# Short convolution's sum and normalised rows kept in PSUM banks, and the low weight parts of one stage fixed on GpSimd

## The chip, the cores and the metric

The kernel runs on one core of a Trainium2 chip. The metric is the device time of one execution in microseconds; the median of several runs is compared. The engines are TensorE (PE), VectorE (DVE), ScalarE (ACT), GpSimd (POOL) and SyncE (SP), which issues most loads. SBUF is the working memory; PSUM has eight banks, each of 128 partitions x 512 float32, into which TensorE writes.

## What is computed

The reference is a block of two layers on 256 tokens with 1024 features, in float32. Only its first stage matters here. Cut to that:

```python
h = rms_norm(x, norm_mix_g)                        # 256 x 1024
proj = h @ w_in                                    # 1024 -> 7168
sc_b, sc_c, sc_x, cf_a, cf_g, gate_sc, gate_cf = split(proj)
y_sc = (sc_b * causal_depthwise_conv(sc_c * sc_x, sc_conv_w)) @ sc_w_out     # short: 3 taps
cf = (cf_a + b1) * sigmoid(cf_g + b2)
cf = silu(layer_norm(causal_depthwise_conv(cf, cf_conv_w) + cf_conv_b))      # long: 31 taps
y_cf = cf @ cf_w_pw2 + cf_b_pw2
x = x + (sigmoid(gate_sc) * y_sc + sigmoid(gate_cf) * y_cf) @ w_mix_out
mem_n = rms_norm(mem, norm_mem_g)                  # keys and values of a cross attention
```

Cross attention, a feed-forward part over 16384 experts and a second block with two attentions follow. All of this is unchanged in the code.

## The kernel before

**Units.** Features lie on the 128 partitions and the 256 tokens along the row. A weight matrix is cut into units of 128 x 1024 float32 (512 KB). A unit is loaded by SP into `w` (three buffers, L322), rounded by ScalarE to a high part `wh` (L288), and the rest, `wl` = `w` - `wh`, is made by GpSimd or VectorE (L292, in `split_gen`). The moving rows are split in the same way into a high and a low part. A product takes 24 matmuls of 128 columns by 256 tokens (`go`, L370 in `blk`): 16 with `wh` and 8 with `wl`. `wh` and `wl` have three buffers each, so the split of a unit waits for the end of the unit three before it.

**Order of the work.** TensorE's order is the order in which the program calls `go`. Everything else is a generator that yields operations, each with an engine, a planned cost and what it depends on. A planner (`Sched`) keeps a planned time for every engine and writes the instructions out one after another; where an operation names two engines (`either`: VectorE or GpSimd) it takes the one that is planned to end first, with a bias added. For `wl` the bias is -2000 ns for GpSimd unless the unit names another. The order is fixed when the program is built, and each engine then runs its own instructions in that order.

**The first stage.** The 56 units of `w_in` come in this order: a and g of the long convolution in turn for j = 0 to 7; then triples c, x, b of the short convolution for j = 0 to 7, with six units of `w_v` (`go_v`, L800 to L804) after the third triple; then the gates gs and gc, 16 units. The first units (j < 4) take `x` times its gain, and their result is multiplied by the row factor `R0` afterwards; from j = 4 on they take the normalised row `hN`. Eight units of `sc_w_out`, eight of `w_k` and eight of `cf_w_pw2` follow.

**The short convolution.** `post_c` copies the c unit's result to `scc` on ScalarE. `post_x` multiplies the x unit's bank by it into `scx` (SBUF, L238), then makes the sum over three taps in `scy` (SBUF): a tensor_scalar (L659) and two products-and-sums (scalar_tensor_tensor, L662), all on VectorE. `post_b` multiplies the b unit's bank by `scy`; ScalarE takes the high part `eA` of it and VectorE the low part `eB`.

**Normalised rows.** `prep_n` and `prep_mem` multiply one of eight tiles of the input or of the memory by its row factor into `mt` (SBUF, two buffers; `either`), and `hl_gain` makes from it the high part on ScalarE and the low part on VectorE (L479): `hN` and `memHL`. They run in two lanes of four tiles.

**Beside it.** The long convolution (`conv_gen`) is 31 steps for each of eight tiles on VectorE, L603 for the first and L607 for the others, with the running sum in a bank; it has a low priority and fills VectorE's planned free time. `layer_norm` adds its tiles up (L717, L739) and needs matmuls with ones (L460 has the same for the row factors `R0` and `Rm`, from square sums `sqT`).

**Banks.** Two pools of four banks each: `mmb` for the results of units, `msb` for the rest. Before the change the first stage uses `msb` for the long convolution (`conv_bank`), for the layer norm's sums (`ln_bank`) and for three later results of the layer norm.

The planned costs that the change exchanges are these, in ns:

```python
def c_dve(n, ap=0, fast=False):
    return 66 + n / (1.92 if fast else 0.96) + 60 * ap
def c_psum(n, ap=0):
    return 130 + n / 0.96 + 40 * ap
```

Of the kernel before, what the change touches and what calls it, by code (L numbers as in the profile page):

```python
# [19 lines left out]
F32 = mybir.dt.float32  # L20
# [5 lines left out]
OP = mybir.AluOpType  # L26
# [4 lines left out]
S = 256  # L31
# [147 lines left out]
# [6 lines that stand above are left out]
# [16 lines left out]
def tile_kernel(ctx, tc, A, out):  # L201
# [24 lines left out]
    def once(pool):  # L226
        b = []

        def f():
            if not b:  # L230
                b.append(pool())
            return b[0]

        return f


    def tt(o, a, b, op):
        return lambda e="dve": ENG[e].tensor_tensor(o, a, b, op=op)  # L238
# [14 lines left out]
    def vcol(name, j=0, w=1):  # L253
        return vec[:, VC[name] + j:VC[name] + j + w]
# [81 lines left out]
    def add(src, **kw):  # L336
        u = dict(src=src, i=len(units), **kw)
        units.append(u)
        return u
# [136 lines left out]
    def hl_gain(H, L, src, g, n, hev, lev, deps=()):  # L476
        yield Op("act", c_act(n, 1), act(H, src, AF.Copy, scale=g), deps=deps, ev=hev)
        yield Op("dve", c_dve(n, 1),
                 lambda: V.scalar_tensor_tensor(L, src, g, H.bitcast(F32), op0=OP.mult, op1=OP.subtract), ev=lev)  # L479
# [77 lines left out]
        yield from rstd(sqT[:, 0], Rm, (), "Rm", bank=mmb)  # L557

    def prep_mem(k):
        t = T1.tile([128, S], F32, tag="mt", bufs=2, name="mt")  # L560
        yield Op(either(S), tt(t, mem[:, k], Rm, OP.mult), deps=["Rm"])
        yield from hl_gain(memHL[:, 0, k], memHL[:, 1, k], t, vcol("norm_mem_g", k), S, None, ("mem", k))

    def mem_part(c):

# [76 lines left out]
    scx, scc = {}, {}  # L642
# [8 lines left out]
    def post_x(j):  # L651
        def g(p):
            b = T1.tile([128, 2 + S], F32, tag="scx", bufs=2, name="scx")
            y = T1.tile([128, S], F32, tag="scy", bufs=3, name="scy")
            scx[j] = y
            yield Op("pool", 40.0, lambda: POOL.memset(b[:, 0:2], 0.0))
            yield Op("dve", c_dve(S), tt(b[:, 2:2 + S], p[:, :S], scc[j], OP.mult), deps=[("scc", j)])
            yield Op("dve", c_dve(S, 1, True),
                     lambda: V.tensor_scalar(y, b[:, 0:S], vcol("sc_w", j * 3), None, op0=OP.mult))  # L659
            for k in (1, 2):  # L660
                yield Op("dve", c_dve(S, 1),
                         lambda k=k: V.scalar_tensor_tensor(y, b[:, k:k + S], vcol("sc_w", j * 3 + k), y,  # L662
                                                            op0=OP.mult, op1=OP.add),
                         ev=("scy", j) if k == 2 else None)
        return g

# [16 lines left out]
    cfHL = P1.tile([128, 2, 8, S], FR, tag="cfHL", name="hN")  # L683

    def prep_n(k):
        t = T1.tile([128, S], F32, tag="mt", bufs=2, name="mt")
        yield Op(either(S), tt(t, x[:, k], R0, OP.mult), deps=["R0"])
        yield from hl_gain(cfHL[:, 0, k], cfHL[:, 1, k], t, vcol("norm_mix_g", k), S, None, ("hn", k))

# [15 lines left out]
    def layer_norm():  # L705
        M0 = T1.tile([128, S], F32, tag="R", bufs=3, name="M0")
        Rl = T1.tile([128, S], F32, tag="R", bufs=3, name="Rl")
        acc = T1.tile([128, S], F32, tag="acc", name="accl")

        def sum1():  # L710
            return ln_bank()[:, 0:S]

        def sum2():
            return ln_bank()[:, S:2 * S]

        for j in range(1, 7):
            yield Op("dve", c_psum(S), lambda j=j: V.tensor_tensor(  # L717
                acc if j == 6 else sum1(), cc[:, j], cc[:, 0] if j == 1 else sum1(), op=OP.add),
                deps=[("cc", 0), ("cc", j)])
        b, c = [None], [None, None]  # L720

        def f():
            b[0] = msb()
            PE.matmul(b[0][:, :S], onesD, acc, start=True, stop=True)

        yield Op("pe", 430.0, f)
        yield Op("act", c_act(S), lambda: ACT.activation(M0, b[0][:, :S], AF.Copy, scale=8.0 / 7.0), ev="M0")
        yield Op("act", c_act(S), lambda: ACT.activation(b[0][:, :S], b[0][:, :S], AF.Copy, scale=8.0 / 7.0))
        acc2 = T1.tile([128, S], F32, tag="acc", name="acc2")
        t7 = T1.tile([128, S], F32, tag="mt", bufs=2, name="t7")  # L730
        sq0 = T1.tile([128, S], F32, tag="t", bufs=4, name="sq0")
        for j in range(8):
            t = t7 if j == 7 else T1.tile([128, S], F32, tag="cfa", bufs=3, name="cm")
            yield Op("dve", c_psum(S), lambda t=t, j=j: V.tensor_tensor(t, cc[:, j], b[0][:, :S], op=OP.subtract),
                     deps=[("cc", j)], chain=False, ev="t7" if j == 7 else None)
            sq = sq0 if j == 0 else T1.tile([128, S], F32, tag="sq", bufs=2, name="sq")
            yield Op("act", c_act(S), act(sq, t, AF.Square), ev="sq0" if j == 0 else None)
            if j:
                yield Op("dve", c_psum(S), lambda j=j, sq=sq: V.tensor_tensor(  # L739
                    acc2 if j == 7 else sum2(), sq, sq0 if j == 1 else sum2(), op=OP.add))  # L740

        def f1():
            c[0], c[1] = msb(), msb()
            ln["mu"], ln["R"] = c[0][:, :S], c[1][:, :S]
            PE.matmul(c[0][:, :S], onesD, t7, start=True, stop=True)
            PE.matmul(c[1][:, :S], onesD, acc2, start=True, stop=True)

        yield Op("pe", 860.0, f1)
        d2 = T1.tile([128, S], F32, tag="cfa", bufs=3, name="d2")
        yield Op("act", c_act(S), lambda: ACT.activation(d2, c[0][:, :S], AF.Square), chain=False)  # L750
        yield Op("dve", c_psum(S), lambda: V.tensor_tensor(d2, c[1][:, :S], d2, op=OP.subtract))
        yield Op("dve", c_psum(S), lambda: V.tensor_tensor(c[0][:, :S], M0, c[0][:, :S], op=OP.add), chain=False,
                 ev="mu")
        yield Op("act", 310.0, lambda: ACT.activation(Rl, d2, AF.Sqrt, bias=epsc[:, 0:1]))
        yield Op("dve", 1670.0, lambda: V.reciprocal(c[1][:, :S], Rl), ev="Rl")
        yield Op("act", 1400.0, lambda: ACT.activation(junk, epsc[:, 0:1], AF.Silu), chain=False)
# [69 lines left out]
        order += [("a", j), ("g", j)]  # L826
    tiles0 = {"b": 0, "c": 8, "x": 16, "a": 24, "g": 32, "gs": 40, "gc": 48}
    for key, j in order:
        u_in[key, j] = add(W["w_in"][tiles0[key] + j])
    VAT, NV1 = 9, 3  # L830
    u_v = []
    order2 = []
# [3 lines left out]
    for i, (key, j) in enumerate(order2):  # L836
        if i == VAT:
            u_v += [add(W["w_v"][n]) for n in range(2 * NV1)]
        u_in[key, j] = add(W["w_in"][tiles0[key] + j])
    u_sc = [add(W["sc_w_out"][n]) for n in range(8)]  # L840
    u_k = [add(W["w_k"][n]) for n in range(8)]
    u_cf = [add(W["cf_w_pw2"][n]) for n in range(8)]
# [1268 lines left out]
```

## Time and profile before

| | us |
|---|---|
| median of 3 runs (lowest, highest) | 1807.87 (1806.69, 1808.79) |
| the profiled execution, its own time | 1811.32 |
| its span, first to last instruction | 1809.5 |
| TensorE busy, matmuls | 1688.5 (93%) |
| VectorE busy | 1222.8 (68%) |
| ScalarE busy | 803.3 (44%) |
| GpSimd busy | 1185.9 (66%) |

All times in the rows are microseconds from the span's start unless they are marked ns; "x8" is a count. An arrow in a tile's name reads "output <- inputs", and "<-ACT wh L288" behind idle time names what ended it. The mean granted TensorE clock of the whole execution is 0.954 of full speed.

### The profile page before, as it was taken

The page shows a single profiled execution, that of the slowest core. Times are in us where ns is not written, and L with a number is a line of the kernel's source. Part 1 is how long each engine was busy: PE and PEld are TensorE (multiplying, and loading weights), DVE is VectorE, ACT ScalarE, POOL GpSimd, SP SyncE. Part 2 cuts the span into 40 slices and gives each one's busy share as a digit, 9 for nine tenths or more (in the row PEclk, how much of TensorE's full clock was granted, in tenths as well). Part 3 has the DMA queues.
Part 4 walks back from the last instruction along what each step waited for, and adds up shares of the span by engine and source line. Part 5 has one row for each costly group of instructions (what it writes and reads, how often), then busy time and mean ns, then how long its engine had stood idle before and what let it go on. Part 6 is the DMA issues. An engine that isn't in the chain of part 4 may idle for free.

```text
span 1809.5 us, 33154 instructions
## 1 busy us (share of the span) xinstructions
PE 1688.5 (93%) x13460; PEld 1666.1 (92%) x13460; DVE 1222.8 (68%) x1994; ACT 803.3 (44%) x1302; POOL 1185.9 (66%) x509
## 2 busy tenths in 40 slices
PE   8898989898996999999999999999999889979997
PEld 7898989898996999999999999999999878979997
DVE  7999966658998706776006777889787897474302
ACT  5533445555443442222443223444444545656533
POOL 5677865456685884444884556887688633768885
PEclk8999999999998998888999999999999999999999
DMA  6454644445453453222553334555455331545553
GB/s 200 151 175 146 192 163 141 129 129 165 148 182 115 150 179 115 94 94 94 171 180 117 115 117 129 186 180 161 152 186 181 120 102 65 165 139 176 185 187 117
DMA packets 75305, 266.73 MB, mean 147 GB/s; under 512 B 8720, under 2 KB 9232, under 8 KB 75152
## 3 DMA queue, kind: packets, MB, share of 16 engines
q1 hardware_dynamic: 73856, 262.77, 44.8%
q8 instruction: 105, 1.72, 0.4%
q10 hardware_dynamic: 1296, 1.85, 0.3%
q14 instruction: 48, 0.39, 0.1%
HBM read 262.48 MB, written 2.10 MB: 146 GB/s over the span
## 4 chain that ended last, share of the span: by engine, by line
PE 61%; DVE 33%; ACT 3%; issue 2%; DMA 1%; POOL 0%; SPq 0%; DVEq 0%; ACTq 0%; POOLq 0%
PE mmb L370 29%; PE msb L1343 7%; PE msb L1341 7%; PE msb L1345 7%; DVE msb L607 5%; PE msb L1264 4%; PE mmb L1264 4%; DVE zz L238 3%; DVE scr L1182 1%; DVE scy L662 1%; DVE scr L1143 1%; DVE scr L1140 1%; ACT wh L288 1%; DVE scr L1179 1%; DVE scr L1142 1%
## 5 line engine op out<-in xcount | busy, mean ns | idle before, releaser
L292 POOL TENSOR_TENSOR wl<-w,wh 128x1024 fp32r<-128x1024 f32 x473 | 1162.2, 2461 | 591.4 <-ACT wh L288 413.3
L288 ACT ACTIVATE wh<-w 128x1024 fp32r<-128x1024 f32 x491 | 518.4, 1059 | 587.9 <-PE msb L1343 260.1
L238 DVE TENSOR_TENSOR zz<-Ah,zz 128x256 fp32r<-128x256 f32 x128 | 216.4, 1693 | 140.0 <-ACT zz L241 140.0
L370 PE MATMUL mmb<-hA,wh 128*128 128x256 f32 x1024 | 263.8, 293 | 1.2 <-ACT wh L288 1.2
L370 PE MATMUL mmb<-hB,wh 128*128 128x256 f32 x1024 | 262.1, 291 | 0.0
L1343 PE MATMUL msb<-zz,wh 128*128 128x256 f32 x1008 | 252.1, 287 | 7.8 <-DVE zz L238 7.7
L1341 PE MATMUL msb<-zz,wh 128*128 128x256 f32 x1008 | 253.2, 288 | 0.8 <-ACT zz L241 0.8
L370 PEld LDWEIGHTS mmb<-hA,wh 128*128 128x128 f32 x1024 | 206.6, 202 | 1.4 <-ACT wh L288 1.4
L370 PEld LDWEIGHTS mmb<-hB,wh 128*128 128x128 f32 x1024 | 205.6, 201 | 0.0
L1343 PEld LDWEIGHTS msb<-zz,wh 128*128 128x128 f32 x1008 | 197.1, 196 | 8.8 <-DVE zz L238 8.8
L1341 PEld LDWEIGHTS msb<-zz,wh 128*128 128x128 f32 x1008 | 197.2, 196 | 1.0 <-ACT zz L241 1.0
L370 PE MATMUL mmb<-hA,wl 128*128 128x256 f32 x1024 | 156.3, 299 | 0.4 <-POOL wl L292 0.4
L1345 PE MATMUL msb<-zz,wl 128*128 128x256 f32 x1008 | 145.0, 287 | 0.0
L370 PEld LDWEIGHTS mmb<-hA,wl 128*128 128x128 f32 x1024 | 142.1, 205 | 0.6 <-POOL wl L292 0.6
L370 PE MATMUL mmb<-hN,wh 128*128 128x256 f32 x896 | 120.4, 286 | 13.3 <-ACT hN L241 5.5
L1345 PEld LDWEIGHTS msb<-zz,wl 128*128 128x128 f32 x1008 | 132.3, 195 | 0.0
L1264 PEld LDWEIGHTS <-ohF 128*128 128x128 f16 x1024 | 121.5, 146 | 11.2 <-DVE ohF L1256 6.0
L370 PEld LDWEIGHTS mmb<-hN,wh 128*128 128x128 f32 x896 | 113.2, 195 | 15.3 <-ACT wh L288 6.7
L607 DVE SCALAR_TENSOR_TENSOR msb<-glu,vec,msb 128x256 f32<-128x256 f32 x232 | 113.1, 487 | 6.2
L1268 DVE SCALAR_TENSOR_TENSOR Ah<-msb,Ah 128x512 f32<-128x512 f32 x32 | 22.1, 692 | 101.3 <-PE msb L1264 101.3
L1234 ACT ACTIVATE Ah<-mmb 128x256 f32<-128x256 f32 x128 | 47.1, 368 | 84.0 <-PE mmb L370 84.0
L370 PE MATMUL mmb<-eu,wh 128*128 128x256 f32 x512 | 70.7, 287 | 6.4 <-DVE uHL L474 2.7
(465 smaller groups left out, 3268.1 us busy)
## 6 DMA issues: line engine op xcount, KB each, us to landing
w<-in_peer_u_dram SPq DMA_DIRECT2D x128, 512.0 KB, 3.5
w<-in_peer_v_dram SPq DMA_DIRECT2D x128, 512.0 KB, 3.5
w<-in_w_in_dram SPq DMA_DIRECT2D x81, 512.0 KB, 3.5
w<-in_w_up_dram SPq DMA_DIRECT2D x32, 512.0 KB, 3.5
w<-in_w_down_dram SPq DMA_DIRECT2D x32, 512.0 KB, 3.5
w<-in_w_peer_q_dram SPq DMA_DIRECT2D x16, 512.0 KB, 3.7
w<-in_w_v_dram SPq DMA_DIRECT2D x8, 512.0 KB, 3.5
w<-in_sc_w_out_dram SPq DMA_DIRECT2D x8, 512.0 KB, 3.6
```

Source lines behind the costliest of these rows:

```text
L238: return lambda e="dve": ENG[e].tensor_tensor(o, a, b, op=op)
L288: yield Op("act", c_act(1024), lambda: ACT.activation(h, w, AF.Copy), deps=u["wdep"], ev=("H", u["i"]))
L292: lambda e: ENG[e].tensor_tensor(l, w, h.bitcast(F32), op=OP.subtract), ev=("L", u["i"]))
L370: PE.matmul(p[:, :S], a, b, start=first and n == 0, stop=last and n == len(todo) - 1)
L607: lambda k=k: V.scalar_tensor_tensor(cc[:, j] if k == 30 else o(), glu[:, j, k:k + S], vcol("cf_w", j * 31 + k), o(), op0=OP.mult, op1=OP. ...
L662: lambda k=k: V.scalar_tensor_tensor(y, b[:, k:k + S], vcol("sc_w", j * 3 + k), y, op0=OP.mult, op1=OP.add),
L1234: yield Op("act", c_act(S), lambda: ACT.activation(Ah[n // 64][:, n % 64], p[:, :S], AF.Gelu), ev=("U", n))
L1264: PE.matmul(b[0][:, t * 64:(t + 1) * 64], ohJ[:, :, t], gI[i][:, :, t], start=i == 0, stop=i == 1)
L1268: yield Op("dve", c_dve(512), lambda: V.scalar_tensor_tensor(z, b[0].rearrange("p (t i) -> p i t", t=8), 1.0 / GS, z, op0=OP.mult, op1=OP. ...
L1341: PE.matmul(o, u["H"][:, d, :], opH, start=first and d % 2 == 0, stop=False, skip_group_check=True)
L1343: PE.matmul(o, u["H"][:, d, :], opL, start=False, stop=False, skip_group_check=True)
L1345: PE.matmul(o, u["L"][:, d, :], opH, start=False, stop=last, skip_group_check=True)
```

## The change

Four things are done.

1. In `post_x` the sum over the three taps is kept in the x unit's own bank `o`; only the last step writes `scy` in SBUF. The planned costs become those of operations on a bank.
2. In `prep_n` and `prep_mem` the product `t` lies in one of two banks of the `msb` pool (`prep_bank`), by the tile's parity, instead of `mt`.
3. The units of `w_in` get a bias of -1e6 ns for GpSimd, so that their `wl` is made by GpSimd alone. (The first unit is split in halves by another function, `split_halves`, which has no bias and stays as it was.)
4. The tag `mt`, now used by one tile of the layer norm alone, has one buffer.

```diff
     def prep_mem(k):
-        t = T1.tile([128, S], F32, tag="mt", bufs=2, name="mt")
+        t = prep_bank[k % 2]()[:, :S]
         yield Op(either(S), tt(t, mem[:, k], Rm, OP.mult), deps=["Rm"])
         yield from hl_gain(memHL[:, 0, k], memHL[:, 1, k], t, vcol("norm_mem_g", k), S, None, ("mem", k))
+
+    prep_bank = [once(msb), once(msb)]
...
             yield Op("pool", 40.0, lambda: POOL.memset(b[:, 0:2], 0.0))
-            yield Op("dve", c_dve(S), tt(b[:, 2:2 + S], p[:, :S], scc[j], OP.mult), deps=[("scc", j)])
-            yield Op("dve", c_dve(S, 1, True),
-                     lambda: V.tensor_scalar(y, b[:, 0:S], vcol("sc_w", j * 3), None, op0=OP.mult))
+            o = p[:, :S]
+            yield Op("dve", c_psum(S), tt(b[:, 2:2 + S], o, scc[j], OP.mult), deps=[("scc", j)])
+            yield Op("dve", c_psum(S, 2),
+                     lambda: V.tensor_scalar(o, b[:, 0:S], vcol("sc_w", j * 3), None, op0=OP.mult))
             for k in (1, 2):
-                yield Op("dve", c_dve(S, 1),
-                         lambda k=k: V.scalar_tensor_tensor(y, b[:, k:k + S], vcol("sc_w", j * 3 + k), y,
-                                                            op0=OP.mult, op1=OP.add),
+                yield Op("dve", c_psum(S, 1),
+                         lambda k=k: V.scalar_tensor_tensor(y if k == 2 else o, b[:, k:k + S],
+                                                            vcol("sc_w", j * 3 + k), o, op0=OP.mult, op1=OP.add),
                          ev=("scy", j) if k == 2 else None)
...
     def prep_n(k):
-        t = T1.tile([128, S], F32, tag="mt", bufs=2, name="mt")
+        t = prep_bank[k % 2]()[:, :S]
...
-        t7 = T1.tile([128, S], F32, tag="mt", bufs=2, name="t7")
+        t7 = T1.tile([128, S], F32, tag="mt", bufs=1, name="t7")
...
     for key, j in order:
-        u_in[key, j] = add(W["w_in"][tiles0[key] + j])
+        u_in[key, j] = add(W["w_in"][tiles0[key] + j], bias=-1e6)
...
-        u_in[key, j] = add(W["w_in"][tiles0[key] + j])
+        u_in[key, j] = add(W["w_in"][tiles0[key] + j], bias=-1e6)
```

## Rows read from the trace of the kernel before

**Rows 1.** The page: chain that ended last, by engine, and the group of splits on GpSimd

```profile
PE 61%; DVE 33%; ACT 3%; issue 2%; DMA 1%; POOL 0%; SPq 0%; DVEq 0%; ACTq 0%; POOLq 0%
...
L292 POOL TENSOR_TENSOR wl<-w,wh 128x1024 fp32r<-128x1024 f32 x473 | 1162.2, 2461 | 591.4 <-ACT wh L288 413.3
```

**Rows 2.** Busy time by stretch: length, PE, PEld, DVE, ACT, POOL, clock, DMA, GB/s

```profile
80.00:128.00 48.00, 43.88 (x366) 42.61 (x365) 44.85 (x80) 18.09 (x24) 37.88 (x21) 1.00 0.52 165
128.00:180.00 52.00, 45.93 (x379) 43.94 (x378) 49.81 (x85) 19.09 (x28) 36.57 (x20) 1.00 0.47 153
180.00:216.00 36.00, 36.00 (x308) 36.00 (x307) 33.65 (x71) 18.42 (x27) 33.29 (x15) 1.00 0.66 211
216.00:240.00 24.00, 19.01 (x136) 18.49 (x135) 22.45 (x47) 7.57 (x11) 8.53 (x5) 0.86 0.37 127
```

**Rows 3.** Waits from 0 to 440 us: us in total, times, longest us

```profile
ACT eA L241 <- DVE mmb L238: 51.2, 8, 6.8
...
PE mmb L370 <- ACT wh L288: 7.7, 6, 2.2
...
PE mmb L370 <- ACT hN L241: 5.5, 1, 5.5
...
PE mmb L370 <- DVE gs L238: 4.2, 1, 4.2
...
PE mmb L460 <- DVE sqT L238: 3.8, 1, 3.8
...
PE mmb L370 <- DVE hN L479: 2.3, 2, 2.0
```

**Rows 4.** VectorE's groups of instructions from 0 to 440 us: busy us, mean ns

```profile
L607 DVE SCALAR_TENSOR_TENSOR msb<-glu,vec,msb 128x256 f32<-128x256 f32 x232 | 113.1, 487 | 6.2
...
L662 DVE SCALAR_TENSOR_TENSOR scy<-scx,vec,scy 128x256 f32<-128x256 f32 x16 | 21.8, 1360 | 0.0
L659 DVE TENSOR_SCALAR scy<-scx,vec 128x256 f32<-128x256 f32 x8 | 11.2, 1402 | 0.9
L479 DVE SCALAR_TENSOR_TENSOR hN<-mt,vec,hN 128x256 fp32r<-128x256 f32 x8 | 10.4, 1326 | 0.0
...
L479 DVE SCALAR_TENSOR_TENSOR memHL<-mt,vec,memHL 128x256 fp32r<-128x256 f32 x8 | 9.3, 1202 | 1.4 <-ACT memHL L241 1.4
...
L603 DVE TENSOR_SCALAR msb<-glu,vec 128x256 f32<-128x256 f32 x8 | 4.4, 546 | 0.3
...
L479 DVE SCALAR_TENSOR_TENSOR pe0b<-mmb,vec,pe0a 128x256 fp32r<-128x256 f32 x8 | 3.7, 478 | 1.6 <-ACT pe0a L241 1.6
...
L717 DVE TENSOR_TENSOR msb<-cc,msb 128x256 f32<-128x256 f32 x4 | 1.7, 426 | 0.1
...
L717 DVE TENSOR_TENSOR msb<-cc 128x256 f32<-128x256 f32 x1 | 1.4, 1418 | 0.0
```

**Rows 5.** ScalarE in order of time, first and last of eight: start, length, idle before

```profile
87.57 0.38 ACT L241 ACTIVATE eA<-mmb 128x256 fp32r<-128x256 f32 x1 [6.62 <-DVE mmb L238]
...
174.90 0.38 ACT L241 ACTIVATE eA<-mmb 128x256 fp32r<-128x256 f32 x1 [6.75 <-DVE mmb L238]
```

**Rows 6.** The first 60 us: GpSimd and VectorE in time; L292 and `mt`, ns min/median/max

```profile
11.76 2.35 POOL L292 TENSOR_TENSOR wl<-w,wh 128x1024 fp32r<-128x1024 f32 x1 [0.62 <-ACT wh L288]
...
14.32 0.68 DVE L238 TENSOR_TENSOR sqT<-sqT 128x512 f32<-128x512 f32 x1
14.92 0.47 DVE L532 SCALAR_TENSOR_TENSOR e0e0b<-x,vec,e0e0a 128x256 fp32r<-128x256 f32 x1
...
L292 DVE TENSOR_TENSOR wl<-w,wh x2: 1215/1216/1218, 16.4 to 30.8; 128x1024 fp32r<-128x1024 f32 x2
...
L238 POOL TENSOR_TENSOR mt<-x,R x1: 743/743/743, 22.9 to 22.9; 128x256 f32<-128x256 f32 x1
```

**Rows 7.** VectorE in order of time, from 183 to 230 us: start, length

```profile
183.22 16.77 DVE L607 SCALAR_TENSOR_TENSOR msb<-glu,vec,msb 128x256 f32<-128x256 f32 x32
...
229.00 0.75 DVE L238 TENSOR_TENSOR gs<-mmb,gs 128x256 f32<-128x256 f32 x2
```

## The prediction

> **What bounds the kernel now.** The page's chain of work [rows 1] gives TensorE 61% of the span and VectorE 33%, so TensorE sets the time except where VectorE feeds it late. The busy time by stretch [rows 2] shows where: from 80 to 180 us TensorE is idle 4.1 + 6.1 = 10.2 of 100 us; from 180 to 216 us, the gates, it is never idle and does 308 matmuls in 36 us, that is 24 x 36 / 308 = 2.81 us for a unit of 24; from 216 to 240 us it is idle 5.0 us and its granted clock is 0.86 of full speed, so part of that stretch runs below the 2.4 GHz level. The waits of the first 440 us [rows 3] name the causes. TensorE waits for `wh` of L288 (7.7 us), for `hN` of L479 early (2.3 us), for the memory's square sums `sqT` (3.8 us), for `gs` (4.2 us) and for `hN` behind the layer norm (5.5 us). The longest other line is ScalarE at `eA`, 51.2 us in eight waits for VectorE's `mmb`: the end of the short convolution's sum.
>
> That last wait explains the idle time from 80 to 180 us. The work runs in triples c, x, b. ScalarE takes its instructions in order; behind `eA` of one triple stands `wh` of a unit two places on, which TensorE then lacks. From the first `eA` to the last [rows 5] are 174.90 - 87.57 = 87.3 us, for seven triples and the six units of `w_v`, 27 units. At 2.81 us they would take 75.9 us. So 11.4 us, or 1.6 us a triple, is lost there; ScalarE waits 51.2 / 8 = 6.4 us each time.
>
> Why the sum is slow stands in VectorE's groups [rows 4]. The long convolution's step (L607), with one tensor in SBUF and one in a bank, takes 0.487 us in 232 cases while GpSimd is 70 to 80% busy beside it [rows 2]. The short convolution's steps, all in SBUF, take 1.402 (L659) and 1.360 us (L662). In the same way the low part of a normalised row takes 1.326 or 1.202 us (L479 `hN`, `memHL`) where its source is in SBUF, and 0.478 us (`pe0b`) where it is in a bank. A sum of two SBUF tensors took 1.418 us although it wrote a bank (L717 `msb<-cc`), against 0.426 us with one of them in the bank. I read from this that a VectorE step with two tensors read from SBUF, or a tensor_scalar from SBUF to SBUF, waits out the GpSimd split in flight (2.461 us, L292 in [rows 1]), and that a bank in place of one input frees it.
>
> **The change part by part.** *The sum.* One tensor_scalar and two products-and-sums for each of 8 tiles move to the x unit's own bank. From 1.402 + 2 x 1.360 = 4.12 us they come to the forms of L603 (0.546 us) and L607 (2 x 0.487 us), 1.52 us: 2.6 us a triple, 20.8 us of VectorE in all. The multiplication in front and the one behind keep their forms. The chain in front of `eA` is thus 2.6 us shorter, and the loss to cover is 1.6 us: TensorE's wait goes and 1.0 us is in hand. Then the triple must fit into 3 x 2.81 = 8.4 us. VectorE's 94.7 us of work between 80 and 180 us fall by 20.8 to 74, GpSimd keeps 74.5 us, and both have 100 - 11.4 = 88.6 us. I take the whole **11.4 us**; below it stands 5.7 (half, if another wait comes up), above it 12. The x bank is held until the last of the sum's steps instead of the first multiplication; its next user is the fourth unit on and the b unit, one later, holds its bank longer already, so nobody new waits.
>
> In [rows 4] the tensor_scalar takes 1.402 us in SBUF and 0.546 into a bank. The Trainium skill speaks against moving it: the page VectorE: DVE Perf Modes, section Why PSUM operands drop a tier, says that fp32 with an operand in a bank loses the mode with two elements a cycle. If the step ran in SBUF at the speed that this suggests, half of 0.546 us as an estimate from that page, the bank would cost 0.27 us more; the products-and-sums alone would shorten the chain by 2 x 0.873 = 1.75 us, 1.5 would be left of it, just below the loss of 1.6, and the sum below would be some 2 us smaller. The rows never show it at that speed, so I keep 2.6.
>
> *The rows of input and memory.* Sixteen low parts go from 1.326 and 1.202 us to the 0.478 of `pe0b`: 8 x 0.848 = 6.8 us of VectorE before 43 us, 8 x 0.724 = 5.8 us before 80 us. ScalarE's high part also reads the bank now; that is a few hundredths and costs nothing, as ScalarE waits for VectorE there. But the product in front (`mt`) still reads two SBUF tensors, and L717 says that such a product waits even when it writes a bank. A wait that the low part took before often falls to the next product now. So the gain lies between 0 and 6.8 us; following the order of both engines, I leave VectorE 4.5 us earlier at the end of the `hN` rows. TensorE's 2.3 us for `hN` go, and of the 3.8 us for `sqT` 2.2: **4.5 us**. The memory rows lie beside TensorE work, which has no idle time from 60 to 80 us; they shift VectorE, not the end.
>
> One of the sixteen products ran on GpSimd, in 0.743 us [rows 6]; the planner may choose either engine. By the Trainium skill, PSUM — Partial Sum Buffer, The four PSUM rules, GpSimd cannot reach a bank. No run here shows that, and by it the product would move to VectorE at 0.43 to 1.42 us. It is small against the bounds that I have given.
>
> *Low parts on GpSimd alone.* VectorE has two such splits of `w_in`, both of 1.22 us, at 16.4 and 30.8 us [rows 6]. GpSimd is free from 11.76 + 2.35 = 14.11 us on, so there the first of them runs from then to about 16.5, just where VectorE wants a two-tensor sum of `sqT` (14.32) and the last low part of x (`e0e0b`, 14.92), which the first unit of TensorE waits for. The sum then ends at 16.5 + 0.68 = 17.2 and `e0e0b` at 17.6 instead of 15.4: **2.2 us later**, between 0 (if VectorE gets in first) and 4.9 (two splits of 2.46). The second split is removed from VectorE at 1.2 us and lets a product wait about as long; nothing. Behind the wait on GpSimd stand only further splits, and its load stays below TensorE's pace, 2.46 against 2.81 us a unit.
>
> *What stays.* From the last triple on, VectorE works through the long convolution at 16.77 / 32 = 0.52 us a step until it reaches `gs` at 229 us [rows 7], 4.2 us late for TensorE. The planner sets how many steps stand there, by costs: the sum is dearer by 0.37 us a tile for it (3.0 us in eight), the two splits go (2 x 1.13 us). So the order moves by under 1 us. VectorE enters this run earlier by the 1.0 us in hand: **1.0 us**, bounds 0 and 4.2. The 5.5 us behind the layer norm hang on a chain in which the long convolution's last tile is interleaved with TensorE's own units; I leave them, bounds a gain of 5.5 and a loss of 2. No load is moved on SP's queue, and later stages have the code of before.
>
> **The sum.** 11.4 + 4.5 - 2.2 + 1.0 = 14.7 us. The profiled execution took 1811.32 us, 1.8 more than its span and 0.2% above the median of 1807.87; from it the sum gives 1796.6, from the median 1793.2. I predict against the median: 1793 us. A measurement here tells a change from none at about 0.2%, 3.6 us.
>
> **The rivals.**
> *Half of it (0.14).* With the sum out of the way, `wh` or `wl` is late for another reason: a load, or a GpSimd split queued behind two others. For it: GpSimd does three splits in 7.4 of 8.4 us. Against it: the gates run at 2.81 us a unit with GpSimd 92% busy. The triples then bring 5.7 us: 1807.9 - 5.7 - 4.5 + 2.2 - 1.0 = 1799.
> *The later stalls go too (0.12).* VectorE is relieved of some 33 us in all. If the planner's order lets that reach `gs` and the layer norm, a further 3.2 + 5.5 us go: 1784.
> *No change (0.07).* The new forms wait as the old did, as L717's 1.418 us into a bank did. Then the sum and rows bring nothing and the start costs 2.2 us: 1806 to 1810. Against it are the 232 cases of L607.
> *Slower (0.05).* GpSimd as the only splitter becomes the bound. The place is L292 from 16 to 216 us: 55 further units of `w_in` and six of `w_v` in 200 us, 3.28 us each. At 2.461 us a split it is far from that; were it held up by VectorE's steps to 3.40 us, 61 x 0.12 = 7 us would be lost: 1815. It decides from 3.28 us on. Against it: it is VectorE that is seen to wait, while 473 splits average 2.461 us.
>
> **How the numbers follow.** The forecast has 0.62, with its own range of 1788 to 1798 from the bounds of its terms. The range 1783 to 1803 takes in the half gain with no help from the rows, and the case where the later stalls go; it leaves out what ends near no change or slower. Faster by over 0.2%: 0.62 + 0.14 + 0.12 = 0.88; the same 0.07; slower 0.05.
>
> **What would show it.** Right: the sum's steps at 0.49 to 0.55 us, `hN` and `memHL` at 0.48, ScalarE's wait at `eA` near 3.8 us, `eA` first to last in about 76 us, TensorE without idle time between 80 and 165 us; the first unit about 2 us later; `gs` still about 3 us late, and 5.5 us behind the layer norm. Wrong: sum steps above 1 us, TensorE waiting for `wl` of L292, or splits above 2.8 us; a first unit that starts no later, or stalls at `gs` and the layer norm that are gone.

## The result, and the profile after

The changed kernel took 1788.68 us (median; lowest 1785.92, highest 1790.33) beside 1808.33 us for the kernel before on the same chip: a ratio of 0.9900, with a 95% interval of 0.9882 to 0.9919, that is 19.65 us less. Measured a second time, beside other kernels, it took 1790.19 us against 1807.78 (0.9908, 0.9888 to 0.9928). The forecast was 1793, its own range 1788 to 1798. Both results lie in it, at the fast end; the profiled execution after took 1789.14 us with a span of 1787.3.

The page of the kernel after: the chain that ended last, by engine, and the splits on GpSimd.

```profile
PE 64%; DVE 30%; ACT 3%; issue 2%; DMA 1%; POOL 0%; SPq 0%; DVEq 0%; ACTq 0%; POOLq 0%
...
L292 POOL TENSOR_TENSOR wl<-w,wh 128x1024 fp32r<-128x1024 f32 x475 | 1168.3, 2462 | 566.7 <-ACT wh L288 387.2
```

Against [rows 1], three points of the chain went from VectorE to TensorE. The split is as long as it was, 2.462 us, so GpSimd is no worse off beside a freer VectorE.

Busy time by stretch, after; columns as in [rows 2].

```profile
80.00:128.00 48.00, 48.00 (x418) 48.00 (x417) 41.20 (x87) 22.93 (x29) 42.49 (x22) 1.00 0.58 199
128.00:180.00 52.00, 52.00 (x462) 52.00 (x461) 47.33 (x103) 24.72 (x36) 45.79 (x22) 1.00 0.56 193
180.00:216.00 36.00, 35.19 (x301) 34.81 (x300) 33.86 (x72) 16.24 (x22) 27.06 (x11) 1.00 0.52 176
216.00:240.00 24.00, 21.54 (x165) 21.28 (x165) 17.57 (x39) 11.42 (x20) 15.38 (x7) 0.93 0.47 157
```

TensorE's idle 10.2 us of [rows 2] between 80 and 180 us are gone, and it does 880 matmuls there instead of 745.

VectorE's groups after, 0 to 440 us: busy us, mean ns.

```profile
L610 DVE SCALAR_TENSOR_TENSOR msb<-glu,vec,msb 128x256 f32<-128x256 f32 x232 | 113.2, 488 | 6.4
...
L238 DVE TENSOR_TENSOR msb<-mem,Rm 128x256 f32<-128x256 f32 x8 | 7.8, 1012 | 0.0
L238 DVE TENSOR_TENSOR msb<-x,R 128x256 f32<-128x256 f32 x8 | 7.1, 884 | 0.1
...
L667 DVE SCALAR_TENSOR_TENSOR mmb<-scx,vec,mmb 128x256 f32<-128x256 f32 x8 | 3.9, 490 | 0.3
L664 DVE TENSOR_SCALAR mmb<-scx,vec 128x256 f32<-128x256 f32 x8 | 3.9, 488 | 1.1 <-POOL scx L659 0.3
...
L667 DVE SCALAR_TENSOR_TENSOR scy<-scx,vec,mmb 128x256 f32<-128x256 f32 x8 | 3.8, 475 | 0.0
...
L479 DVE SCALAR_TENSOR_TENSOR hN<-msb,vec,hN 128x256 fp32r<-128x256 f32 x8 | 3.7, 474 | 0.0
L479 DVE SCALAR_TENSOR_TENSOR memHL<-msb,vec,memHL 128x256 fp32r<-128x256 f32 x8 | 3.6, 476 | 1.8 <-ACT memHL L241 1.8
...
L722 DVE TENSOR_TENSOR msb<-cc 128x256 f32<-128x256 f32 x1 | 1.9, 1920 | 0.0
```

The sum of a tile takes 0.488 + 0.490 + 0.475 = 1.45 us, where [rows 4] had 4.12; the low parts of the rows take 0.47 us where they took 1.33 and 1.20. The products in front of those rows, with two tensors read from SBUF, still take 0.88 and 1.01 us although they now write a bank.

Those means hide two lengths, and the trace of the kernel before shows which step gets which. GpSimd's splits and VectorE's steps of one triple, before: start, length.

```profile
147.98 2.39 POOL L292 TENSOR_TENSOR wl<-w,wh 128x1024 fp32r<-128x1024 f32 x1
...
150.33 2.44 POOL L292 TENSOR_TENSOR wl<-w,wh 128x1024 fp32r<-128x1024 f32 x1
```

```profile
149.36 1.16 DVE L659 TENSOR_SCALAR scy<-scx,vec 128x256 f32<-128x256 f32 x1
...
150.83 2.22 DVE L662 SCALAR_TENSOR_TENSOR scy<-scx,vec,scy 128x256 f32<-128x256 f32 x1
...
153.37 0.47 DVE L662 SCALAR_TENSOR_TENSOR scy<-scx,vec,scy 128x256 f32<-128x256 f32 x1
```

The splits end at 150.37 and 152.77. The first step began inside one split and ends 0.15 us after it, at 150.52; the second ends 0.28 us after the other, at 153.05; the third met no split and takes 0.47 us. So it goes for all 40 steps of the sum and of the low parts of the rows in this trace: 23 begin inside a split and end 0.15 us (tensor_scalar) or 0.28 us (the others) after its end, and the other 17 take 0.47 or 0.48 us. After the change all 24 steps of the sum begin inside a split, and none is held; in one triple:

```profile
144.42 2.40 POOL L292 TENSOR_TENSOR wl<-w,wh 128x1024 fp32r<-128x1024 f32 x1 [0.28 <-ACT wh L288]
```

```profile
144.80 0.49 DVE L664 TENSOR_SCALAR mmb<-scx,vec 128x256 f32<-128x256 f32 x1
145.32 0.49 DVE L667 SCALAR_TENSOR_TENSOR mmb<-scx,vec,mmb 128x256 f32<-128x256 f32 x1
```

What the prediction read from the means, that such a step waits out the split in flight and that a bank in place of one input frees it, is thus there step by step.

The waits after, 0 to 440 us, columns as in [rows 3]; the last line is ScalarE's.

```profile
PE mmb L460 <- DVE sqT L238: 6.0, 1, 6.0
...
PE mmb L370 <- ACT hN L241: 5.5, 1, 5.5
...
PE mmb L370 <- DVE e0e0b L532: 4.4, 5, 1.5
...
PE msb L729 <- DVE accl L722: 2.5, 1, 2.5
...
ACT eA L241 <- DVE mmb L238: 1.3, 5, 0.3
```

Of [rows 3], the 51.2 us at `eA` became 1.3, the waits for `gs` and for `hN` of L479 are gone. The one for `sqT` grew from 3.8 to 6.0 us, the one for `accl` from 0.8 to 2.5.

Four places in TensorE's order give a ruler: the first matmul of the first triple, of the first gate, of the short convolution's output, and of `mge1a`, the stage that follows. First before, then after: start, length.

```profile
71.18 1.98 PE L370 MATMUL mmb<-hN,wh 128*128 128x256 f32 x16
...
166.03 2.10 PE L370 MATMUL mmb<-hN,wh 128*128 128x256 f32 x16 [1.14 <-ACT wh L288]
...
213.73 0.28 PE L370 MATMUL mmb<-eA,wh 128*128 128x256 f32 x1
...
299.76 0.28 PE L370 MATMUL mmb<-mge1a,wh 128*128 128x256 f32 x1
```

```profile
72.26 1.98 PE L370 MATMUL mmb<-hN,wh 128*128 128x256 f32 x16
...
154.82 1.41 PE L370 MATMUL mmb<-hN,wh 128*128 128x256 f32 x11
...
198.34 0.28 PE L370 MATMUL mmb<-eA,wh 128*128 128x256 f32 x1
...
281.53 0.28 PE L370 MATMUL mmb<-mge1a,wh 128*128 128x256 f32 x1
```

After stands against before by +1.1, -11.2, -15.4 and -18.2 us. The last of the four, the start of `mge1a`, is called the mark below. Behind it TensorE's and VectorE's instructions come in the same order in every kernel of this study. There the profiled executions took between 1497.6 and 1512.2 us with nothing changed, and the medians come from executions that differ by as much as 19 us for one kernel. So small effects are read below from the marks, and medians only decide where an interval stands beside them. A mark comes from one trace: two traces of the kernel after differ by 0.7 us in it, and an early clock can make 2.3 us (last section). A difference of under some 3 us is no effect by itself.

### The profile page after: what moved, and what is told of

Read it like the earlier page. It is cut to its first block, busy times and chain, and to the rows that moved or that the text cites. A ratio compares the mean times of both kernels' runs of the same rounds, so it can differ in the third digit from the quotient of the medians.

```text
span 1787.3 us, 33153 instructions
## 1 busy us (share of the span) xinstructions
PE 1676.0 (94%) x13460; PEld 1656.3 (93%) x13460; DVE 1200.1 (67%) x1993; ACT 806.2 (45%) x1302; POOL 1191.6 (67%) x510
## 4 chain that ended last, share of the span: by engine, by line
PE 64%; DVE 30%; ACT 3%; issue 2%; DMA 1%; POOL 0%; SPq 0%; DVEq 0%; ACTq 0%; POOLq 0%
PE mmb L370 33%; PE msb L1348 6%; PE msb L1346 6%; PE msb L1350 6%; DVE zz L238 6%; PE msb L1269 4%; PE mmb L1269 4%; DVE msb L610 3%; DVE scr L1187 1%; DVE ohF L1256 1%; DVE scr L1148 1%; DVE scr L1145 1%; DVE scr L1184 1%; ACT zz L241 1%; DVE scr L1147 1%
## 5 line engine op out<-in xcount | busy, mean ns | idle before, releaser
L292 POOL TENSOR_TENSOR wl<-w,wh 128x1024 fp32r<-128x1024 f32 x475 | 1168.3, 2462 | 566.7 <-ACT wh L288 387.2
L238 DVE TENSOR_TENSOR zz<-Ah,zz 128x256 fp32r<-128x256 f32 x128 | 220.6, 1725 | 137.4 <-ACT zz L241 137.3
L370 PE MATMUL mmb<-hN,wh 128*128 128x256 f32 x896 | 116.4, 281 | 5.5 <-ACT hN L241 5.5
```

Of the source, the lines that this page charges most:

```text
L292: lambda e: ENG[e].tensor_tensor(l, w, h.bitcast(F32), op=OP.subtract), ev=("L", u["i"]))
L370: PE.matmul(p[:, :S], a, b, start=first and n == 0, stop=last and n == len(todo) - 1)
```

## The experiments

The last two columns are the start of the first triple and of `mge1a` in the trace, us; before they are 71.2 and 299.76, after 72.3 and 281.53.

| kernel | median us | ratio to before (95%) | first triple | `mge1a` |
|---|---|---|---|---|
| before + sum in the bank | 1790.31 | 0.9900 (0.9869 to 0.9932) | 71.2 | 281.58 |
| after, sum in SBUF again | 1803.86 | 0.9965 (0.9946 to 0.9985) | 72.6 | 293.76 |
| before + low parts on GpSimd alone | 1808.80 | 1.0011 (0.9994 to 1.0028) | 72.3 | 297.10 |
| before + rows in banks | 1801.38 | 0.9965 (0.9947 to 0.9984) | 67.5 | 291.62 |
| before, `eA` on VectorE | 1821.58 | 1.0077 (1.0052 to 1.0101) | 70.7 | 312.02 |
| after, start free again | 1787.32 | 0.9886 (0.9865 to 0.9908) | 69.3 | 277.45 |
| after, square sums later | 1784.13 | 0.9867 (0.9841 to 0.9894) | 67.4 | 277.10 |
| after, long convolution priced higher | 1813.28 | 1.0026 (1.0009 to 1.0043) | 72.2 | 303.96 |
| after, unaltered | 1790.19 | 0.9908 (0.9888 to 0.9928) | 72.3 | 280.79 |
| before + sum, planned at old costs | 1785.98 | 0.9889 (0.9866 to 0.9912) | 68.8 | 275.89 |
| sum and rows, square sums later | 1781.98 | 0.9878 (0.9853 to 0.9902) | 62.7 | 272.84 |
| after, long convolution priced lower | 1791.20 | 0.9914 (0.9894 to 0.9935) | 72.1 | 280.72 |

**The sum alone.** The kernel before with the change's first part and nothing else:

```diff
...
-            yield Op("dve", c_dve(S, 1, True),
-                     lambda: V.tensor_scalar(y, b[:, 0:S], vcol("sc_w", j * 3), None, op0=OP.mult))
+            yield Op("dve", c_psum(S, 2),
+                     lambda: V.tensor_scalar(o, b[:, 0:S], vcol("sc_w", j * 3), None, op0=OP.mult))
...
```

> The kernel before with the short convolution's sum alone moved to the bank. Theory 1 (the sum holds ScalarE's in-order queue, so the wh splits behind eA come late): the triples and gates run without waits, some 15 us less than before, 1791 to 1795 us, eA waits under 1 us each. Theory 2 (the gain is VectorE's relief in all, the rows as much as the sum): about half of the 20 us, 1797 to 1800 us.

1790.31 us, and the mark at 281.58, where the whole change has 281.53. The sum by itself brings what the change brings, a little more than was expected of it. `eA` still waits 6.4 us in all, up to 2.6 in the first triples.

**Everything but the sum**, the same edit taken out of the kernel after.

> The changed kernel with the sum put back in SBUF; rows in banks and low parts on GpSimd stay. Theory 1: the loss at eA is back, TensorE idle about 10 us between 80 and 180 us, within 4 us of before, 1805 to 1811 us. Theory 2: half of the gain stays, 1797 to 1800 us.

1803.86 us, a little under the range. `eA`'s waits are back at 47.6 us, `gs` at 5.2. The rest of the change is worth 6.0 us by the mark when the sum is absent, and nothing when it is there (281.58 against 281.53).

**Low parts on GpSimd alone.** The kernel before with:

```diff
-        u_in[key, j] = add(W["w_in"][tiles0[key] + j])
+        u_in[key, j] = add(W["w_in"][tiles0[key] + j], bias=-1e6)
```

> The kernel before with the bias alone: w_in's low parts on GpSimd only. If the split that follows the first one holds up the last low part of x: e0e0b of the first unit about 2 us later and the time 1809 to 1812 us. If GpSimd taking two splits relieves VectorE more than it costs: 1805 to 1807 us.

1808.80 us, no change that can be told, between the two ranges. The first triple comes 1.1 us later, the mark 2.7 earlier (297.10 against 299.76): TensorE waits 2.3 us for `hN` behind the layer norm in this order, instead of 5.5.

**`eA` on VectorE.** The kernel before; the high part of the short convolution's output is copied by VectorE, so that nothing on ScalarE waits for it. The sum stays in SBUF.

```diff
-            yield from hl(eA[:, j], eB[:, j], y_, S, None, ("ysc", j))
+            yield Op("dve", c_psum(S), lambda: V.tensor_copy(eA[:, j], y_))
+            yield Op("dve", c_dve(S), tt(eB[:, j], y_, eA[:, j].bitcast(F32), OP.subtract), ev=("ysc", j))
```

> The kernel before, with eA (the high part of the short convolution's result) copied by VectorE instead of ScalarE; the sum stays in SBUF at 4.1 us. Theory 1: nothing holds ScalarE's queue any more, TensorE's idle time from 80 to 180 us falls below 4 us though VectorE has 8 x 0.42 = 3.4 us more to do; 1794 to 1800 us. Theory 2 (VectorE's amount of work bounds the triples): nothing gained or 3 us lost, 1807 to 1812 us.

1821.58 us, slower by 0.77%, and outside both ranges. Nothing on ScalarE waits for the sum any more, and yet no time came back: the wait moved. From this kernel's waits (0 to 440 us), its busy time by stretch, and VectorE's groups from 80 to 180 us:

```profile
PE mmb L370 <- DVE eB L238: 13.5, 4, 4.5
```

```profile
128.00:180.00 52.00, 41.90 (x337) 41.37 (x335) 49.82 (x74) 17.30 (x22) 36.53 (x20) 0.93 0.46 154
```

```profile
L662 DVE SCALAR_TENSOR_TENSOR scy<-scx,vec,scy 128x256 f32<-128x256 f32 x16 | 31.7, 1981 | 0.0
L659 DVE TENSOR_SCALAR scy<-scx,vec 128x256 f32<-128x256 f32 x8 | 8.2, 1022 | 0.9
```

TensorE now waits for `eB`, for a bank of the triple to come free. VectorE is busy 95.7 of the 100 us from 80 to 180, against 94.7 before. The copies took 3.4 us of it, and the sum itself got longer: its products-and-sums take 1.981 us against 1.360 in [rows 4], the tensor_scalar 1.022 against 1.402, together 16 x 0.62 - 8 x 0.38 = 6.9 us more on an engine that has little to spare. The edit thus gave VectorE some 10 us of work besides clearing ScalarE's queue, and the clock of 0.93 says that part of the stretch ran below the 2.4 GHz level, behind waits of up to 4.5 us; the size of the loss is no measure of the queue alone. That VectorE sets the pace shows in the kernel before as well. From 80 to 180 us VectorE waits for another engine once; this is its whole list of waits there:

```profile
DVE vHL L238 <- ACT vHL L241: 1.0, 1, 1.0
```

After the change the same list comes to 6.4 us. VectorE bounds the triples before; ScalarE's queue was the road by which its lateness reached TensorE.

**Rows in banks alone.** The kernel before with the change's second part (both products fixed on VectorE).

> The kernel before with only the normalised rows of input and memory kept in banks (their products always on VectorE), the sum in SBUF, low parts shared as before. Prediction's step: TensorE's 2.3 us for hN and 2.2 of its 3.8 us for sqT go, 1803 to 1804 us. Rival, from the trace after: hN's wait goes, but the wait at the memory's square sums (3.8 us before, 6.0 after) grows by about as much, so 1806 to 1809 us, no change. hN and memHL at 0.48 us each in both; eA's waits stay at 6.4 us each.

1801.38 us, 6.7 less than before, and 8.1 us by the mark: the rival fell (the wait for `sqT` is 4.4 us, not 6), and by itself this part is worth more than the prediction's 4.5 us. The first triple starts 3.7 us earlier, the first gate 6.6 (159.40 against 166.03). With the low parts on GpSimd alone beside it, as in the whole change, the first triple starts 1.1 us later than before. Those 4.8 us are the subject of the next two runs. ScalarE in order of time, first with the rows alone, then after the whole change: start, length, idle time before.

```profile
42.75 1.06 ACT L288 ACTIVATE wh<-w 128x1024 fp32r<-128x1024 f32 x1 [1.43 <-DMA w<-in_w_in_dram]
43.72 1.66 ACT L542 ACTIVATE sqT<-mem 128x512 f32<-128x512 f32 x3
```

```profile
44.64 1.06 ACT L288 ACTIVATE wh<-w 128x1024 fp32r<-128x1024 f32 x1 [3.51 <-DMA w<-in_w_in_dram]
...
47.39 1.65 ACT L542 ACTIVATE sqT<-mem 128x512 f32<-128x512 f32 x3
```

In the second, `wh` waits for a tile's load that lands 1.9 us later, and the memory's squares, behind it and one more `wh` in ScalarE's order, start 3.7 us later. They feed the 6.0 us wait at L460.

**The start free again.** The kernel after; the first three low parts of `w_in` may go to VectorE, and one of them does (1.22 us at 16.2). The product of the input's rows, which ran on VectorE in the kernel after, is fixed there.

```diff
-        yield Op(either(S), tt(t, x[:, k], R0, OP.mult), deps=["R0"])
+        yield Op("dve", c_dve(S), tt(t, x[:, k], R0, OP.mult), deps=["R0"])
...
-    for key, j in order:
-        u_in[key, j] = add(W["w_in"][tiles0[key] + j], bias=-1e6)
+    for i, (key, j) in enumerate(order):
+        u_in[key, j] = add(W["w_in"][tiles0[key] + j], bias=-2000.0 if i < 3 else -1e6)
```

> The changed kernel with the first splits of w_in free to go to VectorE again (the product of the input's rows is fixed on VectorE). If the 2 us by which the first unit came later reach the end of the span: 1786.5 to 1787 us, with e0e0b's last at about 15 us in place of 16.9. If they are swallowed at TensorE's wait for sqT (6.0 us after, it would then be about 8): 1788 to 1790 us, no change against the changed kernel, and the first triple starts at 72.3 us as before.

The first triple starts at 69.3 instead of 72.3, the mark stands at 277.45, 4.1 us earlier (3.3 against the second trace of the kernel after), and `sqT` costs 5.0 instead of 6.0 us. So the price of the third part at the start is carried through to the mark, as far as one trace tells. The median, 1787.32 us, can't tell 1.4 us from none.

**The square sums' matmul later.** The kernel after; TensorE takes L460 of the memory 2.5 units later.

```diff
-        yield from rstd(sqT[:, 0], Rm, (), "Rm", bank=mmb)
+        yield from rstd(sqT[:, 0], Rm, ["memwait"], "Rm", bank=mmb)
...
+        sch.ev["memwait"] = t + 11500.0
         sch.spawn(stat_mem(), ready=t, prio=400.0)
```

> The changed kernel with the matmul of the memory's square sums placed 2.5 units later in TensorE's order. Theory (rows' gain is lost in the wait of 6.0 us at this matmul): the wait goes, the first triple starts up to 6 us earlier, and without a new wait the time is 1783 to 1784 us. Rival: the memory rows are now late for the first unit of go_v or VectorE is, so TensorE waits a few us there instead: 1786 to 1789 us.

1784.13 us, and the mark at 277.10, 4.4 us earlier. The 6.0 us became 1.1; 2.1 us for `glu` appeared, and nothing later on. The first triple gains 4.9 us, more than the 2.8 that the waits lose (6.0 less 1.1 and 2.1); the lower clock goes with the wait. The stretch behind it, first after the whole change, then here, columns as in [rows 2]:

```profile
56.00:63.00 7.00, 5.80 (x25) 5.65 (x26) 6.37 (x11) 3.18 (x4) 2.42 (x2) 0.51 0.23 80
```

```profile
56.00:63.00 7.00, 4.33 (x34) 3.76 (x34) 6.79 (x10) 4.71 (x7) 6.99 (x4) 1.00 0.54 171
```

Behind the wait of 6.0 us TensorE runs there at the 1.2 GHz level and does 25 matmuls; here it stays at 2.4 GHz and does 34 in less busy time.

**The long convolution priced higher.** The same instructions; only the planner's numbers differ.

```diff
-        yield Op("dve", c_psum(S, 2),
+        yield Op("dve", c_psum(S, 2) + 100.0,
...
-            yield Op("dve", c_psum(S, 1),
+            yield Op("dve", c_psum(S, 1) + 85.0,
```

> The changed kernel with the planner's costs of the long convolution's steps raised by 100 and 85 ns, near the 522 ns that they take; the work is the same, only the order shifts by a few steps. If the order set by these costs is what leaves VectorE behind at accl and cc (TensorE waits there 2.5 us after): 1785 to 1787 us. If not: 1788 to 1790 us, with the wait moved to another line.

1813.28 us: 24.6 us lost, 22.4 of them ahead of the mark, with no instruction changed. A price nearer to the truth for one kind of step made the planner put fewer of them into each triple; VectorE's busy time from 128 to 180 us fell to 43.85 from 47.33, and the long convolution's tail came late. Waits from 0 to 440 us:

```profile
PE msb L750 <- DVE t L739: 16.5, 1, 16.5
...
PE msb L729 <- DVE accl L722: 9.2, 1, 9.2
```

**Priced lower**, by 60 ns a step, the reverse:

> The changed kernel with the planner's costs of the long convolution's steps lowered by 60 ns, the reverse of the run that raised them (1813.3 us). The steps then end earlier and accl's and the layer norm's matmuls move some units forward in TensorE's order. If VectorE has room for them in the triples: the waits at accl (2.5 us) and hN behind the layer norm (5.5 us) shrink, 1780 to 1786 us. If it has not (47.3 of 52 us busy there): eB or the banks come late, TensorE waits in the triples, 1790 to 1800 us.

1791.20 us, with the mark at 280.72, as after. The 5.5 us for `hN` behind the layer norm go, and `accl`, now earlier in TensorE's order, takes 10.2 us. The time lies in the second range, but not for its reason: the triples kept their pace without a wait, and the stall only changed its name.

**The changed kernel unaltered**, beside these:

> The changed kernel unaltered, beside the three kernels of this call, so that they can be compared on one chip: 1787 to 1790 us by its first measurement of 1788.7. The span behind the first matmul on mge1a (1505.8 us in its first trace) shows how far that part differs from one execution to the next.

1790.19 us; the mark at 280.79, 0.7 us from the first trace, and 1505.2 us behind it.

**The sum at the old costs.** The kernel before; the sum in the bank, the planner told that it costs what it did in SBUF.

```diff
...
-            yield Op("dve", c_psum(S, 2),
+            yield Op("dve", c_dve(S, 1, True),
                      lambda: V.tensor_scalar(o, b[:, 0:S], vcol("sc_w", j * 3), None, op0=OP.mult))
...
```

> The kernel before with the sum in the x unit's bank, but the planner still told the old costs, so that every engine keeps the order of before and only the form of 24 instructions differs. If the form alone does it: about 1790 us, as the run with the sum and its costs had (1790.3), eA's waits gone, and the wait for gs as there. If the order that the new costs bring has a part in it: 1794 to 1800 us, with the waits at gs or accl back at 4 us or more.

1785.98 us, a little under what was expected: the form alone does it. TensorE and VectorE take their instructions in the order of before. Its mark stands 5.7 us ahead of the first run's, of which 2.3 are there at the first triple already (below, an early clock). The other 3.4 arise behind the gates, where the order differs; the waits there come to 9.8 us in the first run and 8.7 here, and what makes the rest is not shown. The medians don't tell the two apart.

**Sum and rows, the square sums later, no third part** (both products of the rows fixed on VectorE).

> The changed kernel without its third part (low parts again free to go to VectorE), and with the memory's square sums' matmul placed 2.5 units later. If the start is worth what the traces show at the first triple (4 us) on top of the placement (4 to 5 us): 1780 to 1782 us, the first eA at about 77 us. Rival: what is won ahead of the first triple is lost at later waits (hN behind the layer norm, accl), and it stays at the 1784 us of the placement alone.

1781.98 us, 0.9878 of before (0.9853 to 0.9902); on the same chip the unaltered change took 1790.19. The mark stands at 272.84, 8.0 us ahead of that kernel's 280.79, as the medians stand 8.2 us apart. This version is the fastest by its median and by the mark; its interval and that of the unaltered change (0.9888 to 0.9928) still overlap by a little, so by the medians alone it would not be settled. What is won ahead of the first triple (72.3 to 62.7) is carried to the mark in all but 1.6 us. Part of that is clock, as with the square sums later alone: from 40 to 72 us it is 1.00 here and 0.89 after the whole change.

## Why the prediction was right, step by step

**The sum.** Right in its form and its size for the triples. From the first triple's start to the last one's end TensorE took 93.7 us before (71.18 to 164.90) and 82.7 after (72.26 to 154.98): 11.0 us against the 11.4 taken. The steps' times were met within 0.06 us. That 11.0 and 11.4 lie so close is luck in part. By the sum's own ruler, first `eA` to last, 87.3 us became 72.9: 14.4 us. The 11.4 had set units of 2.81 us against it, and they ran at 2.72; and of the 14.4 only 11.0 show in TensorE's triples; the other 3.4 are ScalarE's lag behind them, which grew before and shrank after. Two sentences of it failed. One is "ScalarE's wait at `eA` near 3.8 us": it is 0.3 at most (up to 2.6 and 3.1 in the first triples of the two runs with the sum alone). I had treated 6.4 us as the length of the chain, less 2.6; the run with `eA` on VectorE and VectorE's list of waits show that it was the backlog of a full engine, and with 20.8 us taken from that engine the backlog is gone, not shortened. The other is the end of the loss. I let it end with the last triple; but the last `eA` of before stood at 174.90 [rows 5], 10 us behind TensorE's last triple, and `wh` for the first gates was queued behind it. From the end of the triples (9.9 us ahead) to the end of the gates (15.4 ahead) 5.5 us more were gained. That is the term that was left out, and with the others below it makes the 14.7 of the sum into 18.2 at `mge1a`: 14.7 - 0.4 (triples) + 5.5 (gates) - 3.4 (start and rows) + 1.8 (`gs`).

Of the 5.5 us, 12 gates x 0.11 = 1.3 are pace, which may be chance (last section). "2.81 us a unit" was read from the gates of one execution. After, a unit takes 2.72 us there, and in three runs with the sum still in SBUF too, once their stalls are past; `eA` first to last took 72.9 us instead of "about 76" mostly for the same reason.

**The rows.** Predicted 4.5 us, between 0 and 6.8; alone they gave 3.7 at the first triple and 8.1 at the mark, above the bound. That the memory rows "shift VectorE, not the end" failed there: 2.9 of the 8.1 us are won between the first triple and the first gate, where VectorE bounds. What the rest is, no run shows. The reading of L717 was right: `msb<-x,R` and `msb<-mem,Rm` wait in front of a bank as they did in front of SBUF. `hN`'s 2.3 us went as forecast.

**Low parts on GpSimd alone.** Predicted +2.2 us, between 0 and 4.9, and at the first triple it is +1.1 without the rows and +4.8 with them. The first link was right to 0.3 us: the last `e0e0b` ends at 17.34, where 17.6 was forecast. GpSimd and VectorE after, in order of time:

```profile
11.15 4.91 POOL L292 TENSOR_TENSOR wl<-w,wh 128x1024 fp32r<-128x1024 f32 x2
```

```profile
10.10 6.24 DVE L532 SCALAR_TENSOR_TENSOR e0e0b<-x,vec,e0e0a 128x256 fp32r<-128x256 f32 x3
16.27 0.68 DVE L238 TENSOR_TENSOR sqT<-sqT 128x512 f32<-128x512 f32 x1
16.87 0.47 DVE L532 SCALAR_TENSOR_TENSOR e0e0b<-x,vec,e0e0a 128x256 fp32r<-128x256 f32 x1
```

The second split runs until 16.06, the three low parts beside it take 2.1 us each, and the last `e0e0b` starts at 16.87 instead of 14.92. What I missed is the second price: the later splits hold their tiles longer, a load lands late, and ScalarE's squares stand behind the `wh` that waits for it. That the buffer, not the transfer, is what comes late is my reading of the order; no run changed the number of buffers. The net of rows and start was predicted at -2.3 us and is +1.1 at the first triple. This step failed, by 3.4 us, and the gates' 5.5 hid it in the sum; that the total came out close is luck to that extent.

**What stays.** The layer norm's 5.5 us stayed, 5.5 after. `gs` lost all its 4.2 us instead of 1.0, but `accl` grew by 1.7 and a wait of 0.7 us for `wl` appeared; from the gates' end to `mge1a` 2.8 us were gained. (Of the 7.7 us for `wh` in [rows 3], 2.2 lie behind the mark, and they stay, 2.3 after.) Of the sentence that the order moves by under 1 us, the runs with other prices show the weakness: 85 to 100 ns a step moved the end by 25 us, so the size of a price says little of the size of its effect.

**The rivals.** "Half of it" and "no change" fell with the first run. "The later stalls go too" fell, as 5.5 us behind the layer norm stand in both. "Slower" needed splits of 3.28 us; they take 2.46. The Trainium skill's rule that spoke against the bank (VectorE: DVE Perf Modes, Why PSUM operands drop a tier) would have had the tensor_scalar slower there; it is faster, 0.488 against 1.402 us. Where no split is in the way the rule holds: with `eA` on VectorE five of the eight tensor_scalars met none and took 0.35 us from SBUF to SBUF, less than into a bank. Their shortest, median and longest time, in ns, in that run:

```profile
L659 DVE TENSOR_SCALAR scy<-scx,vec x8: 352/355/2344, 81.3 to 171.4; 128x256 f32<-128x256 f32 x8
```

Beside a GpSimd that is busy three quarters of the time, the wait outweighs the 0.13 us.

## What to carry to other kernels

On an engine that is busy 95% of a stretch and itself waits for nobody, a wait further down is a backlog: moving the waiting instruction elsewhere moves the wait (slower by 0.77%), and taking work off the full engine removes it altogether. Here that work was not arithmetic but waiting for another engine's 2.46 us instruction, and one operand in a bank ended it. Follow a late engine's effect past the stage in which it arises, as far as the next queue that it fills, and measure each part of a change by itself and beside the others. In the whole change the low parts on GpSimd cost what the rows had won, which neither part shows alone. And look at single steps before trusting a mean: 1.360 us was never the length of one.

## What was not expected of the hardware

**Two paces at one clock.** TensorE in order of time, the first 16 matmuls of a gate, before and then after:

```profile
188.29 2.05 PE L370 MATMUL mmb<-hN,wh 128*128 128x256 f32 x16
```

```profile
160.26 1.98 PE L370 MATMUL mmb<-hN,wh 128*128 128x256 f32 x16
```

and the same engine by stretch, granted clock 1.00 in both, 257 matmuls in 30 us and 338 in 38:

```profile
183.00:213.00 30.00, 30.00 (x257) 30.00 (x256) 28.00 (x58) 15.96 (x24) 27.98 (x13) 1.00 0.65 206
```

```profile
160.00:198.00 38.00, 38.00 (x338) 38.00 (x337) 35.51 (x74) 18.55 (x29) 33.59 (x15) 1.00 0.57 194
```

A gate takes 2.83 or 2.72 us, one or the other for a dozen units on end, and the same kernel can change from one to the other at a stall: with rows alone the gates begin at 2.83 and go on at 2.72. Two executions of the kernel after part in it as well: the six units ahead of the mark take 2.82 us each in the first trace and 2.71 in the second, which is the 0.7 us between their marks. Nothing in the rows names the cause; it stays open.

**When the clock rises.** The first 22 us, before and in the run of the sum at old costs, whose order is the same there:

```profile
0.00:22.00 22.00, 17.34 (x76) 15.15 (x77) 13.48 (x16) 11.29 (x19) 9.61 (x13) 0.77 0.66 226
```

```profile
0.00:22.00 22.00, 17.70 (x95) 15.95 (x96) 14.96 (x18) 13.34 (x21) 11.60 (x15) 1.00 0.67 225
```

In the second the matmuls follow each other by 0.12 us from 15.6 us on, behind a wait of 1.6 us for `e0e0b`; in the first by 0.21 us until 19.4 us, behind a wait of 1.3 us one `e0e0b` earlier. The last `e0e0b` is done at 15.4 us in both, and from there on the same matmuls put the next L460 at 19.45 and 17.66, 1.8 us apart, and the first triple 2.3, by no work of the kernel's. In the first the granted clock is 0.50, the 1.2 GHz level, from 12 to 20 us; in the second it is given as 1.00 throughout, though from 8.9 to 13.4 us the matmuls follow each other by 0.21 us there too.

**A wait that is no constant.** The same SBUF form took 1.360 us in the kernel before and 1.981 us with `eA` on VectorE, with GpSimd busy 74.5 and 78.3 of 100 us; into a bank it took 0.47 to 0.49 us in every run. The two means are mixtures: 8 of 16 steps met a split before, 13 of 16 there, and each of those ends 0.28 us after the split does. A mean read from one order doesn't hold in another. The Trainium skill (SBUF — State Buffer, SBUF: two separate sides) says that a VectorE instruction with two SBUF inputs and a GpSimd instruction that reads SBUF exclude each other for the length of whichever began first; the steps that begin inside a split agree, each one held until 0.28 us after its end. The single-input tensor_scalar waits here as well, until 0.15 us after; the page has that for VectorE's two-port modes.
